# Sixty filler matmuls of a hybrid block moved from the end of the recurrence to two earlier places

## The chip, the cores and the metric

The kernel runs on one core of a Trainium2 chip. The metric is the device time of one execution in microseconds (us). The engines are named as the profile names them: PE (TensorE matmul), PEld (its weight loads), DVE (VectorE), ACT (ScalarE), POOL (GpSimd), SP (the queue that issues most loads).

## What is computed

One transformer block over 512 tokens of width 1024, all in float32. The part around the change is the mixing half:

```python
z = xn @ w_in                                  # 4640 columns, split below
y_attn = sliding_window_attention(rope(q), rope(k), v, sinks)
r, k, v, w_lo, a_lo, g_lo = split(token_shift(z[..., o3:o4], mu))
# per head, one step per token:
#   sa    = state @ (-kk_t)
#   state = state * w_t + sa (kk_t*a_t)^T + v_t k_t^T
#   y_t   = state @ r_t
merged = sigmoid(z_ga) * (y_attn @ proj_attn) + sigmoid(z_gr) * (y_rwkv @ proj_rwkv)
h = x + merged @ w_out
```

Behind it come a normalisation and a product-key expert layer (scores, top 16, gathered experts), which take most of the time and are not touched.

## The kernel before, in words

**Projections.** The columns of `w_in` are cut into 36 tiles of 128. `z_tile` (L767) computes one: 8 slices of the width, each as three matmuls on split operands (`steps`, L761: low by high, high by low, high by high), so 24 matmuls of 128x512 with moving operand `xh`/`xl`, into one of two PSUM tiles named `mm`. Its weights come in two halves through `weights` (L130): a load on SP's queue into `wraw` (4 buffers), a copy on ACT (`wh` or `wxh`, L139), and the remainder on POOL or DVE (`wl` or `wxl`, L140). Two sets of `wh`/`wl` and two of `wxh`/`wxl` rotate, so a weight half is prepared when PE has left the fourth half before it. `weights` stands under a raised priority.

**Recurrence.** The eight heads are four pairs (`NPAIR`), the 512 tokens eight chunks of 64. For a pair `c`:
- `z_part` (L1138) projects `kT`, `rT`, `vT` (two buffers each). The end of each tile is `shifted` (L1110): an ACT copy out of PSUM into `zt` (two buffers, L1117, raised priority), a DVE subtraction into `zd` (one buffer, L1119), and a DVE multiply-add into `kT`, `rT` or `vT` (L1120).
- `lora_part`, `norm_part` (L1146, L1162) make decay, rate and norm: small matmuls, ACT tanh, and a POOL power between two small DVE steps (`head_rsqrt`, L1095).
- `expand` (L1166): four transposes (L1107), then some 15 DVE operations, 6 POOL operations (L1190, L1200, L1201) and ACT exponentials that end in `SA`, `BK`, `BH`.
- `gram` (L1204): transposes of `vT` (L1213), products of `BK` and `SA` (L1227) that DVE masks into `PB` and `SA` (L1235, L1236), more products (L1240, L1251, L1254, L1258, L1259), and DVE's `XY` and `bon` (L1243 to L1256).
- `levels` (L1263): five doubling levels, each two rounds of matmuls (L1275, L1289) with DVE in between (`V1`, L1278; `XY`, L1292). `expand(c + 1)` is issued inside the third.
- `chain` (L1295): eight chunk steps, each four small rounds of matmuls (L1317, L1323, L1329, and the read L1309, L1311) with DVE and ACT copies between them.
- `fin1`, `fin2`, `fin3` (L1336 to L1358): group normalisation of the pair's output, a chain PE, DVE, ACT, PE, DVE, POOL, DVE, PE, DVE. `fin2` and `fin3` of pair `c` are issued in the `gram` stage of pair `c + 1`; those of the last pair stand at the end.

**Order.** In `phase_mix` PE's order is the order of the program text (a manual schedule for PE alone). DVE, ACT, POOL and SP are ordered by a planner from priorities and estimated times. PE's waits are filled by hand: `filler` (L869) is a generator that yields after each projection matmul but the last of a sum, and `F(n)` (L887) takes `n` such steps. A tile of 24 matmuls is 23 steps, since its last matmul goes with the next tile's first. The filler's order: `z_part(1)`, two `gate_r` tiles, `z_part(2)`, two `gate_r`, `z_part(3)`, four more `gate_r`, eight `gate_a` (the first five with 12 matmuls of `proj_attn`; the last three are projections alone, 72 matmuls in 69 steps). `need(c)` (L883) drives it until pair `c` is projected. After attention (132 steps) the text before has `expand(0)`, `F(24)`, and per pair: 2 steps in `gram`, 2 and 11 behind it, 3 and 4 in each of five levels, 3 and 3 in each chain step (no second 3 in the last), and 6 and 6 around `fin1`. Then `F(FE)` with 6, `fin2` of the last pair, `drain(fill)` (all that is left), and `fin3`.

**Behind it** `merge` (L208) first issues 36 matmuls of `proj_attn` for three late tiles (L219 to L221, from `yaTh`/`yaTl`), and then the `proj_rwkv` matmuls, which need all four pairs' `yrh`/`yrl`.

Of the kernel before, what the change touches and what calls it, by code (L numbers as in the profile page):

```python
# [29 lines left out]
NPAIR = 4  # L30
# [59 lines left out]
def hybrid_block_kernel(ctx, tc, a, out, dbg=None):  # L90
# [54 lines left out]
    with tc.tile_pool(name="xp", bufs=1, reuse_waits="tile") as xp:  # L145
        xh = xp.tile([P, KD, T], F32R, name="xh")
        xl = xp.tile([P, KD, T], F32R, name="xl")
        with ExitStack() as st:
            st.enter_context(tc.manual_schedule(engines={mybir.EngineType.PE}))
            phase_mix(tc, a, dump, mm3, split, ident, mhalf, ps, weights, xh, xl, mga, tgr, rstd_rows)  # L150
# [595 lines left out]
def phase_mix(tc, a, dump, mm3, split, ident, mhalf, ps, weights, xnh, xnl, mga, tgr, rstd_rows):  # L746
    nc = tc.nc
    V, S, G, PE = nc.vector, nc.scalar, nc.gpsimd, nc.tensor
    with ExitStack() as st:
# [7 lines left out]
        def drain(gen):  # L757
            for _ in gen:
                pass
# [123 lines left out]
        def need(c):  # L883
            while c not in ready:
                next(fill)

        def F(n):  # L887
            for _ in range(n):
                next(fill, None)
# [6 lines left out]
        with tc.tile_pool(name="rp", bufs=2, reuse_waits="tile") as rp:  # L896
            rw.rp = rp
            rw.expand(0)
            F(24)
            for c in range(NPAIR):  # L900
                rw.gram(c, F)
                F(FG[0])
                if c:
                    rw.fin2(c - 1)
                F(FG[1])
                if c:
                    rw.fin3(c - 1)
                if c + 1 < NPAIR:
                    need(c + 1)
                    rw.lora_part(c + 1)  # L910
                    rw.norm_part(c + 1)
                rw.levels(c, c + 1 if c + 1 < NPAIR else None, F)
                rw.chain(c, F)
                F(FF)
                rw.fin1(c)
                F(FF)
            F(FE)
            rw.fin2(NPAIR - 1)
            drain(fill)
            rw.fin3(NPAIR - 1)  # L920
# [528 lines left out]
```

## Time and profile before

| | |
|---|---|
| median of three runs | 1825.45 us (1820.81 to 1827.6) |
| the profiled execution, its own time | 1818.6 us |
| its span in the trace | 1816.7 us |
| mean granted PE clock over the span | 0.978 of full speed |
| PE busy | 1714.3 us, 94% |
| DVE busy | 1349.0 us, 74% |
| POOL busy | 780.5 us, 43% |
| ACT busy | 720.4 us, 40% |

Times in rows are microseconds from the span's start. In a row of the timeline the columns are start, length, engine, line, operation, output and inputs, tile size, count, and in brackets the engine's idle time before it with what ended it. A matmul's length overlaps the next one's, so a rate is read from starts. A windows row gives a stretch, its length, and each engine's busy time and number of instructions, then the granted clock (1.00 is 2.4 GHz, 0.50 is 1.2 GHz), the busy share of the DMA engines and GB/s.

### The profile page before, as it was taken

To read this page: it belongs to the slowest core of one execution; us is meant where nothing else is said; L and a number is where in the kernel's file an instruction comes from. 1 tells how busy PE (TensorE), PEld (TensorE's weight loads), DVE (VectorE), ACT (ScalarE), POOL (GpSimd) and SP (SyncE) were. 2 spreads that over 40 slices of the span, in tenths; PEclk is the share of its full clock that TensorE was granted. 3 is DMA by queue.
4 is the path that set the end of the run, shared out by engine and by line. 5 is a ranking of instruction groups with operands and counts; after the bars stand their busy time and mean duration, and the time that the engine had idled before them with its cause. 6 is when DMAs were issued, how large, how long until landed. Compare 5 with 4: busy or idle time off the path is not lost.

```text
span 1816.7 us, 30025 instructions
## 1 busy us (share of the span) xinstructions
PE 1714.3 (94%) x10933; PEld 1432.8 (79%) x10933; DVE 1349.0 (74%) x2564; ACT 720.4 (40%) x1415; POOL 780.5 (43%) x634
## 2 busy tenths in 40 slices
PE   7998899899999789898799999999999999998998
PEld 6765666667778668676689999999999999997886
DVE  4667665754535999999677777677788788788886
ACT  4553132221335436666633333333333333333334
POOL 5534232311155412122255555555455555556450
PEclk9998899999999889999899999999999999999999
DMA  6221111111564225563799999999989999998864
GB/s 210 81 64 41 36 42 48 36 48 54 184 205 133 88 76 178 199 216 142 243 320 325 305 313 325 317 303 317 321 302 318 322 302 320 327 309 290 297 222 167
DMA packets 193397, 378.98 MB, mean 209 GB/s; under 512 B 18624, under 2 KB 65472, under 8 KB 190176
## 3 DMA queue, kind: packets, MB, share of 16 engines
q1 hardware_dynamic: 97344, 175.71, 28.5%
q0 software_dynamic: 36864, 134.23, 22.1%
q10 hardware_dynamic: 59040, 67.12, 10.9%
q8 instruction: 86, 1.41, 0.3%
q14 instruction: 63, 0.52, 0.1%
HBM read 342.12 MB, written 33.55 MB: 207 GB/s over the span
## 4 chain that ended last, share of the span: by engine, by line
PE 45%; DVE 3%; issue 1%; DMA 1%; ACT 0%; POOL 0%; DVEq 0%; SPq 0%; POOLq 0%; ACTq 0%
PE w L96 8%; PE w L97 8%; PE w L98 8%; PE mm L96 7%; PE mm L98 7%; PE mm L97 7%; DMA vraw<-v_t 1%; DVE al L102 1%; DVE gacc L416 1%; DVE vl L102 0%; DVE wxl L102 0%; ACT w L467 0%; DVE gt L466 0%; DMA wraw<-v_t 0%; DVE wl L102 0%
## 5 line engine op out<-in xcount | busy, mean ns | idle before, releaser
L140 POOL TENSOR_TENSOR wl<-wraw,wh 128x512 fp32r<-128x512 f32 (+1 forms) x95 | 133.1, 1401 | 347.4 <-ACT wh L139 292.8
L96 PE MATMUL w<-vh,al 128*128 128x512 f32 x678 | 265.1, 391 | 6.8 <-DVE al L102 6.7
L97 PE MATMUL w<-vl,ah 128*128 128x512 f32 x678 | 264.6, 390 | 0.0
L98 PE MATMUL w<-vh,ah 128*128 128x512 f32 x678 | 264.4, 390 | 0.0
L399 POOL DMA_INDIRECT grow<-v_t,idxV x128 | 175.8, 1373 | 185.3 <-DVE gacc L416 152.1
L352 ACT ACTIVATE big<-mm 128x384 f32<-128x384 f32 x128 | 63.0, 492 | 464.6 <-PE mm L98 372.6
L399 POOL DMA_INDIRECT grow<-u_rows,idxU x128 | 167.9, 1312 | 183.4 <-DVE grow L406 164.3
L140 DVE TENSOR_TENSOR wl<-wraw,wh 128x512 fp32r<-128x512 f32 x101 | 103.8, 1028 | 153.2 <-ACT wh L139 128.4
L96 PE MATMUL mm<-x2h,wl 128*128 128x384 f32 (+1 forms) x576 | 199.2, 346 | 7.6 <-ACT big L352 6.2
L98 PE MATMUL mm<-x2h,wh 128*128 128x384 f32 (+1 forms) x576 | 191.7, 333 | 0.0
L97 PE MATMUL mm<-x2l,wh 128*128 128x384 f32 (+1 forms) x576 | 191.7, 333 | 0.0
L139 ACT ACTIVATE wh<-wraw 128x512 fp32r<-128x512 f32 (+1 forms) x196 | 122.4, 624 | 133.1 <-PE mm L763 53.0
L416 DVE SCALAR_TENSOR_TENSOR gacc<-grow,act,gacc 128x1024 f32<-128x1024 f32 x127 | 166.2, 1309 | 2.2
L102 DVE TENSOR_TENSOR vl<-vraw,vh 128x512 fp32r<-128x512 f32 x217 | 147.8, 708 | 25.5 <-ACT vh L101 25.1
L96 PEld LDWEIGHTS w<-vh,al 128*128 128x128 f32 x678 | 127.6, 188 | 33.3 <-DVE al L102 9.9
L365 POOL TENSOR_TENSOR big<-big,gt 128x384 f32<-128x384 f32 x128 | 135.8, 1064 | 34.3 <-ACT gt L576 21.2
L406 DVE SCALAR_TENSOR_TENSOR grow<-grow,xg 128x1024 f32<-128x1024 f32 x128 | 150.1, 1217 | 0.0
L98 PEld LDWEIGHTS w<-vh,ah 128*128 128x128 f32 x678 | 127.4, 188 | 26.8
L97 PEld LDWEIGHTS w<-vl,ah 128*128 128x128 f32 x678 | 127.5, 188 | 23.0
L96 PE MATMUL mm<-x2h,wxl 128*128 128x384 f32 (+1 forms) x436 | 143.5, 329 | 0.0
L97 PE MATMUL mm<-x2l,wxh 128*128 128x384 f32 (+1 forms) x436 | 143.4, 329 | 0.0
L98 PE MATMUL mm<-x2h,wxh 128*128 128x384 f32 (+1 forms) x436 | 143.4, 329 | 0.0
(388 smaller groups left out, 3944.0 us busy)
## 6 DMA issues: line engine op xcount, KB each, us to landing
wraw<-u_t SPq DMA_DIRECT2D x256, 256.0 KB
vraw<-v_t SPq DMA_DIRECT2D x217, 256.0 KB
g_dram<-stg ACTq DMA_DIRECT2D x24, 1024.0 KB
gt<-g_dram ACTq DMA_DIRECT2D x60, 384.0 KB
wraw<-wz SPq DMA_DIRECT2D x72, 256.0 KB
wraw<-v_t SPq DMA_DIRECT2D x39, 256.0 KB
wraw<-wq SPq DMA_DIRECT2D x32, 256.0 KB
wraw<-wproj SPq DMA_DIRECT2D x16, 256.0 KB
```

The lines of the kernel that those rows point to most:

```text
L96: PE.matmul(o, ll, rh, start=start, stop=False)
L97: PE.matmul(o, lh, rl, start=False, stop=False)
L98: PE.matmul(o, lh, rh, start=False, stop=stop)
L102: V.tensor_sub(lo, src, hi.bitcast(F32))
L139: S.activation(wh[:, :, :m], raw[:, :, :m], AF.Copy)
L140: lo.tensor_sub(wl[:, :, :m], raw[:, :, :m], wh[:, :, :m].bitcast(F32))
L352: S.activation(H[e], o, AF.Gelu)
L365: G.tensor_mul(ht, ht, g[:, :, e % E2B, :])
L399: G.indirect_dma_start(out=r, out_offset=None, in_=src, in_offset=bass.IndirectOffsetOnAxis(ap=idx[:, i:i + 1], axis=0))
L406: V.scalar_tensor_tensor(r, r, 1.0, xg, op0=ALU.mult, op1=ALU.mult, accum_out=hpre[:, s:s + 1])
L416: V.scalar_tensor_tensor(gacc, r, act[:, i:i + 1], gacc, op0=ALU.mult, op1=ALU.add)
```

## The change

The text calls `F(54)` where it called `F(24)`, and `F(10)` before `levels` of the first three pairs, behind `lora_part` and `norm_part` of the next pair. The filler itself is the same, so it ends 60 steps earlier.

```diff
             rw.expand(0)
-            F(24)
+            F(54)
             for c in range(NPAIR):
                 rw.gram(c, F)
                 F(FG[0])
...
                     need(c + 1)
                     rw.lora_part(c + 1)
                     rw.norm_part(c + 1)
+                if c + 1 < NPAIR:
+                    F(10)
                 rw.levels(c, c + 1 if c + 1 < NPAIR else None, F)
                 rw.chain(c, F)
                 F(FF)
```

## Rows read from the trace of the kernel before

**Rows 1.** The page's head: the span, and the granted PE clock in 40 equal slices of 45.4 us (tenths of full speed).

```profile
span 1816.7 us, 30025 instructions
...
PEclk9998899999999889999899999999999999999999
```

**Rows 2.** The windows view: four stretches of 5 us. Columns: stretch, length, then busy time (and instructions) of PE, PEld, DVE, ACT and POOL, granted clock, DMA share, GB/s.

```profile
155.00:160.00 5.00, 0.46 (x2) 0.49 (x2) 4.91 (x5) 0.72 (x1) 4.30 (x3) 0.54 0.17 52
160.00:165.00 5.00, 4.09 (x24) 2.95 (x25) 4.91 (x8) 0.00 (x0) 0.90 (x2) 0.50 0.00 0
...
185.00:190.00 5.00, 4.39 (x67) 3.42 (x65) 1.43 (x4) 0.63 (x1) 0.00 (x0) 0.66 0.13 49
...
210.00:215.00 5.00, 4.67 (x20) 2.71 (x20) 1.69 (x6) 1.33 (x3) 0.78 (x1) 0.50 0.16 52
```

**Rows 3.** PE's timeline around the first pair's `gram`.

```profile
152.46 0.60 PE L1213 MATMUL w<-ident,vT 128*128 128x128 f32 x4
159.54 0.76 PE L1227 MATMUL w<-SA,BK 64*128 64x128 f32 x2 [6.48 <-DVE BK L1199]
161.22 2.04 PE L1227 MATMUL w<-SA,BK 64*128 64x128 f32 x14 [0.91 <-DVE BK L1199]
```

**Rows 4.** DVE's timeline in the same stretch: the end of `expand(0)`, and the first and last masked product of `gram(0)`.

```profile
153.59 1.75 DVE L1198 TENSOR_TENSOR BK<-kk,encum 64x512 f32<-64x512 f32 x1
...
157.04 0.69 DVE L1198 TENSOR_TENSOR BK<-kk,encum 64x512 f32<-64x512 f32 x1
157.76 3.31 DVE L1199 TENSOR_TENSOR BK<-av,encum 64x512 f32<-64x512 f32 x2
...
163.33 0.67 DVE L1235 TENSOR_TENSOR PB<-w,mgram 64x512 f32<-64x512 f32 x1
...
171.19 0.67 DVE L1256 TENSOR_TENSOR bon<-w,vT 128x512 f32<-128x512 f32 x1
```

**Rows 5.** POOL's timeline there: two weight remainders, the second with POOL's idle time before it.

```profile
154.87 1.59 POOL L140 TENSOR_TENSOR wl<-wraw,wh 128x512 fp32r<-128x512 f32 x1
...
173.47 1.28 POOL L140 TENSOR_TENSOR wxl<-wraw,wxh 128x512 fp32r<-128x512 f32 x1 [10.46 <-ACT wxh L139]
```

**Rows 6.** PE's timeline in the levels: five rounds that PE waited for (pair 0 in the first three, then pair 1 and pair 2).

```profile
184.53 0.68 PE L1275 MATMUL w<-XY,PB 64*64 64x64 f32 x16 [2.85 <-DVE XY L1292]
...
185.82 0.88 PE L1275 MATMUL w<-XY,PB 64*64 64x64 f32 x16 [0.61 <-ACT cum L1184]
...
208.40 1.15 PE L1289 MATMUL w<-XY,V 64*64 64x64 f32 x32 [1.85 <-DVE V L1278]
...
265.08 0.68 PE L1275 MATMUL w<-XY,PB 64*64 64x64 f32 x16 [1.55 <-DVE XY L1292]
...
342.31 1.37 PE L1275 MATMUL w<-XY,PB 64*64 64x64 f32 x32 [3.03 <-ACT lw L1181]
```

**Rows 7.** DVE's timeline in the levels of pair 0: the preparation of pair 1, the first `XY`, and the token shift of pair 2's `vT`.

```profile
179.56 1.48 DVE L1101 COPY hw<-hv 128x512 f32<-128x512 f32 x1 [0.51 <-POOL hv L1099]
180.97 1.75 DVE L1180 TENSOR_TENSOR lw<-cum,lw 128x512 f32<-128x512 f32 x1
...
183.79 0.68 DVE L1292 TENSOR_TENSOR XY<-w,XY 128x512 f32<-128x512 f32 x1
...
193.25 1.33 DVE L1119 TENSOR_TENSOR zd<-zt 128x512 f32<-128x512 f32 x1
```

**Rows 8.** PE's timeline at the end of the recurrence: last chain step, `fin1`, `fin2`, `fin3`'s transposes, and `merge`'s first `proj_attn` and first `proj_rwkv` matmul.

```profile
457.54 0.33 PE L1323 MATMUL w<-U,XY 64*64 64x64 f32 x4
...
460.71 1.02 PE L1342 MATMUL w<-yT,blk 128*128 128x512 f32 x2
...
464.56 0.95 PE L1091 MATMUL w<-blk,fin 128*128 128x2 f32 x8
...
475.02 0.60 PE L1107 MATMUL w<-ident,hw 128*128 128x128 f32 x4
475.37 0.48 PE L96 MATMUL w<-yaTh,wxl 128*128 128x512 f32 x1
...
483.86 0.40 PE L96 MATMUL w<-yrh,wl 128*128 128x512 f32 x1
```

**Rows 9.** The windows view of the filler's line (L763) alone, from the last chain step to `merge`, and of `drain(fill)`. Columns: stretch, length, busy time and number of PE and PEld, granted clock, DMA share, GB/s.

```profile
457.54:475.37 17.83, 15.98 (x64) 11.79 (x64) 1.00 0.47 152
465.37:475.02 9.65, 9.65 (x42) 7.78 (x42) 1.00 0.72 237
```

**Rows 10.** DVE's timeline at the end of the recurrence.

```profile
458.17 0.23 DVE L1325 COPY UV<-w 64x64 f32<-64x64 f32 x1 [0.68 <-ACT UV L1324]
461.77 0.69 DVE L1343 SCALAR_TENSOR_TENSOR yT<-w,yT 128x512 f32<-128x512 f32 x1 [3.38 <-PE w L1342]
465.55 0.17 DVE L1098 TENSOR_SCALAR hv<-w 128x8 f32<-128x8 f32 x1 [3.08 <-PE w L1091]
467.46 0.63 DVE L1101 COPY hw<-hv 128x512 f32<-128x512 f32 x1 [1.75 <-POOL hv L1099]
...
479.87 0.68 DVE L102 TENSOR_TENSOR yrl<-yr,yrh 128x512 fp32r<-128x512 f32 x1
```

**Rows 11.** ACT's timeline there: the square of `fin1`.

```profile
462.49 0.63 ACT L1345 ACTIVATE fin<-yT 128x512 f32<-128x512 f32 x1 [2.06 <-DVE yT L1343]
```

**Rows 12.** POOL's timeline there: the power of `fin2`.

```profile
465.79 1.63 POOL L1099 TENSOR_TENSOR hv<-hv,mhalf 128x8 f32<-128x8 f32 x1 [0.38 <-DVE hv L1098]
```

## The prediction, made before the changed kernel ran

> **What bounds the kernel now.** I read the page's head first: PE's granted clock is at its upper level nearly all the time, and the slices below it lie in the first quarter and a few places later [rows 1]. The windows view of the first quarter says where: about 155 to 165 us, 185 to 190 and 210 to 215 the granted clock is 0.50 to 0.66, each time at or behind a stretch in which PE stood [rows 2]. PE's timeline then names the waits. In front of `gram(0)` PE stands 6.48 and 0.91 us for the last `BK` of `expand(0)` [rows 3], and DVE, which makes it, is busy 4.91 of every 5 us there [rows 2]: `expand(0)` and `gram(0)` are paced by DVE. In the levels PE waits for DVE's `XY` or `V1` again [rows 6]. At the end of the recurrence it is the other way round: the granted clock is 1.00, filler matmuls stand back to back (42 in `drain(fill)`, 9.65 us or 0.23 us each, 64 in all from the last chain step to `merge`) [rows 9], and the normalisation chain runs hidden beneath them. So PE bounds the end, DVE the two places to which the change brings work.
>
> **What moves.** 60 filler steps are nearly 63 matmuls (24 matmuls are 23 steps): 31 at `F(54)`, 10.4 at each `F(10)`, 63 fewer at the end. At 0.23 us that is 7.1 us, three times 2.4 us, and 14.4 us. The change removes no work; it can gain only as far as the moved matmuls fall into waits, and as far as what they leave behind can close up. Of the 64 fillers behind the last chain step one or two are left.
>
> **F(54).** PE now comes to the transposes of `vT` at 159.5 instead of 152.46, and to the first `BK` product at about 160.1; its two operands were there at 159.54 and 161.22 [rows 3]. The 7.1 us fit into 7.4 us of waiting. The lower clock that followed costs nothing today, since DVE goes from `BK` through the masked products (163.33) to `bon` (171.19) without a gap that PE caused [rows 4]; curing it gains nothing. What is moved along: PE leaves two weight halves some 15 us earlier, so SP's loads, ACT's copies and POOL's remainders come earlier. POOL's remainder at 173.47, after 10.46 us of idle POOL, and the next one would then fall into 154 to 162 [rows 5], beside the `BK` products. Of two equal `BK` products the one took 1.75 us and the other 0.69 us [rows 4], so a collision costs DVE 1.06 us. From below the cost is zero (POOL's work lands between DVE's operations; a gain is excluded, as DVE has no idle time to close). From above DVE stands for both remainders, 1.59 and 1.28 us [rows 5], and does the token shift's subtraction for `rT(2)` in front of `BK` (0.69 us, as the short `BK`): 3.6 us. I take one collision, **+1.1 us**.
>
> The Trainium skill (SBUF — State Buffer, Who interferes with whom) says that a VectorE instruction with two SBUF inputs and a GpSimd one that reads SBUF exclude each other for a whole instruction; by that both remainders count in full and this term would be +2.9 us. The rows show the stretch of 1.06 us but not what lay on POOL at each start, so the sum keeps 1.1.
>
> **Token shifts.** With 40 more steps done by the end of `levels(0)`'s entry, the shift of `vT(2)` (1.33 us for its subtraction, in the DVE-paced third level [rows 7]) falls to the neighbourhood of `gram(0)`. Its targets are free only late: `rT(2)` overwrites `rT(0)`, read by L1254 in `gram(0)`, and `vT(2)` overwrites `vT(0)`, read by `bon` at 171.19 [rows 4]. PE doesn't wait for this, because ACT's copy empties `mm` first. DVE's relief in the third level on is set against the wait of 1.85 us there [rows 6] and the 5 us at the lower clock behind it [rows 2], worth 2.5 us: at best -4.4, at worst 0 (the planner fills the room with other work of `expand(1)`). I take **-1.5 us**, a third, since 1.33 us is less than the wait.
>
> **F(10), three times.** Each puts 2.4 us of PE work between `norm_part(c + 1)` and the first level. What is queued behind it is the level's matmuls, and DVE's `V1` and `XY` for them; meanwhile DVE can do the preparation of the next pair, which today stands in front of the first `XY` (`hw` 1.48, `lw` 1.75 us, then `XY` at 183.79) [rows 7]. Pair 0: the waits are 2.85 and 0.61 us [rows 6], and at 0.66 in 185 to 190 [rows 2] two thirds of 5 us run at half rate, which costs 1.7. Best 2.4 - 5.2 = -2.8; worst +2.4, if DVE keeps its order and only starts later. I take **-1.5**: most of the wait and half the clock. Pair 1: 1.55 us of wait [rows 6], no clock: between +0.9 and +2.4, I take **+0.9**. Pair 2: 3.03 us [rows 6], like pair 0: best 2.4 - 3.0 - 1.7 = -2.3, worst +2.4, I take **-1.5**.
>
> **The end.** The cover goes, so what is late next is the chain itself, and PE's order makes `merge`'s 36 `proj_attn` matmuls wait behind `fin3`'s transposes. From L1323 at 457.54 [rows 8], by starts: `UV` copied at 458.40 [rows 10]; the read and its ACT copy some 0.9 (an estimate: a small round of 0.33 us [rows 8] and twice the 0.23 us of such a copy [rows 10]); L1342 to DVE 1.06 [rows 8, 10]; to ACT's square 0.72 [rows 10, 11]; the square 0.63 and a hand-over 0.1; L1091 to DVE 0.99 [rows 8, 10]; to POOL 0.24 [rows 10, 12]; to `hw` 1.67 [rows 10, 12]; `hw` 0.63 and 0.1; L1107 to L96 0.35 [rows 8]. With the 0.86 to 458.40 that is 8.2 us, against 17.83 us today: -9.6 us. `yrl` of the last pair came 4.0 us before its first use [rows 8, 10] and moves with `fin3`, so the second half of `merge` waits for nothing new.
>
> Two costs come off it. PE works for some 3 of these 8 us, and behind the wait of 6.48 us its clock was 0.54 and then 0.50 all through 160 to 165, although PE was busy for 4.09 of 5 us [rows 2, 3]. So the chain's own matmuls take about 1 us more, and the `proj_attn` matmuls run some 5.5 us at half rate, 2.7 us lost; twice that as a bound. And weight remainders for `merge`, now early, can stand in front of a DVE step of the chain: one, 0.7 us, by the like `yrl` [rows 10]. **-9.6 + 3.7 + 0.7 = -5.2 us**, between -9.6 and -2.5.
>
> The Trainium skill (TensorE: Matmul & The Clock Gate, Loop structure matters more than you think) speaks against this part: bursts separated by waits run at the lower of the two rates, matmuls standing back to back do not. By it the 2.7 us are due; without it the end would give 7.9.
>
> **The sum.** 1.1 - 1.5 - 1.5 + 0.9 - 1.5 - 5.2 = -7.7 us on the profiled execution's 1818.6 us (span 1816.7), so 1810.9. That execution lies 6.85 us under the median of 1825.45, and I carry the difference over: 1817.8 us. All best ends give -18.2, all worst +8.3. Behind 484 us PE stays the pace until the top-16 work, and that waits for scores, so I let the shift pass on whole. A measurement of this kernel tells some 0.5%, 9.1 us, from no change.
>
> **Rivals.**
> - *Clock and waits both cured*: the planner uses each 2.4 us for the next pair's preparation, the levels' waits and their slow stretches go, the shift of `vT(2)` pays 3 us. 0 - 2.8 + 0.9 - 2.3 - 3 - 5.2 = -12.4: 1813. For it: DVE has the preparation at hand when `norm_part` is through. Against: those orders come from estimates, and POOL's power stands in the middle of the preparation (0.51 us of DVE's wait [rows 7]). Chance 0.25.
> - *Slower: DVE's order in the levels stays.* Place: DVE's queue behind the first `V1`. If `hw` and `lw` stay queued behind `V1`, DVE waits 2.4 us longer for L1275 and then does the same work before `XY`, so every `F(10)` is paid in full. 3.6 + 7.2 + 0 - 5.2 = +5.6: 1831. It decides from the point where two of the three levels keep the wait. For it: `V1` is raised in priority. Against: `V1` can't be planned before PE delivers it. Chance 0.15.
> - *The filler can't be moved at no cost*: ACT's copy of `vT(2)` into `zt` needs the shift of `kT(2)` to be over; if it is queued ahead of ACT's `UV` copies, DVE's first steps of `gram(0)` stand some 3 us (an estimate: from the transposes, now at 160, to the first masked product's 163.33 [rows 4], by which that shift is over), and with the relief gone the sum is -7.7 + 3 + 1.5 = -3.2: 1822. Chance 0.10.
>
> The forecast has 0.50. Range: down to all-best, 1807; up, since the slower rival holds 0.15, to 1829. Faster by over 0.5% takes the first rival and a little of the forecast's tail: 0.31. Slower by as much needs the slower rival near all its worst ends: 0.09. Within: 0.60.
>
> **What would show it.** In the changed trace: no wait above 1 us before L1227 of pair 0 and a clock of 1.00 there; the first-level waits of pairs 0 and 2 under 1 us; 63 fewer L763 matmuls behind the last L1323, 8 to 10 us from there to the first L96, and a granted clock near 0.5 in it. It is wrong if L1227 of `gram(0)` starts later than about 163, if the levels' waits are as long as before, or if the end closes up to more than 13 us.

## The result, and the profile after

The change makes the kernel slower: 1832.07 us (median of 13 runs, 1830.21 to 1840.29) beside 1821.79 us for the kernel before (13 runs, 1818.63 to 1827.6), a ratio of 1.0062 with a 95% interval of 1.0049 to 1.0074. That is some 11 us, outside the predicted range and of the other sign. The span of the profiled execution is 1829.1 us, 12.4 us over that of before.

Behind the two added lines the line numbers of this kernel are 2 higher than before (L1107 is L1109, L1278 is L1280, L1289 is L1291); the experiments keep the old ones.

The granted PE clock of the kernel after in 40 slices, from the page's head, beside [rows 1]:

```profile
PEclk9999989999899989999799999999999999999999
```

Four slices lie below nine tenths, five did before, and they are others: this view doesn't show the loss. Where the time went is read from PE's first matmul of each stage. The table gives each stage's length before and what it is longer in the changed kernel and in six experiments (worked out from the starts in PE's timeline; stages run from the first `expand(0)` transpose over each pair's first L1151, L1317 and L1342 to the last chain step's L1323 and the first `yrh` matmul). Four of the executions measured for the experiments were slower by far, the profiled one of e10 (F(10) in pair 0) among them at 5814.03 us; the ratios leave them out, and the column for pair 0 is read from e15, the same kernel.

| stage | before, us | after | F(54) | three F(10) | F(10), pairs 1 and 2 | F(10), pair 0 | F(34) | F(34), fin2 raised |
|---|---|---|---|---|---|---|---|---|
| expand(0), gram(0) | 28.2 | +3.6 | +3.5 | -0.1 | +0.6 | +0.5 | +0.2 | +0.3 |
| lora to chain, pair 0 | 36.6 | +2.7 | -2.3 | +5.3 | +0.1 | +3.9 | -0.6 | -0.7 |
| chain 0 | 27.7 | -0.4 | +2.4 | +1.8 | -2.2 | +3.0 | +1.9 | +1.1 |
| gram(1) | 16.9 | +3.0 | +0.8 | +3.5 | 0 | +2.2 | +3.4 | +0.6 |
| lora to chain, pair 1 | 33.7 | +3.2 | +1.4 | +5.9 | +7.0 | +5.5 | +5.7 | +4.4 |
| chain 1, gram(2) | 42.4 | +0.4 | 0 | -0.9 | -0.8 | -0.8 | -0.8 | -0.7 |
| lora to chain, pair 2 | 36.6 | +2.5 | -0.2 | +4.4 | +0.6 | -1.5 | -0.6 | -1.6 |
| chain 2 to the last step | 89.2 | +0.7 | +0.1 | +0.1 | +1.0 | +1.8 | +1.8 | +1.8 |
| the end, to `yrh` | 26.3 | -5.7 | -6.4 | -6.4 | -4.7 | -2.3 | -2.3 | -2.2 |
| sum | | +10.0 | -0.7 | +13.6 | +1.6 | +12.3 | +8.7 | +3.0 |

The other 2.4 us of the span after lie ahead of `expand(0)` (1.2) and behind the first `yrh` matmul (1.2), in parts that the change leaves alone.

How far can one trace of each kernel be compared? e14, which moves no matmul, has each of these stages within 0.5 us of before, but is 1.1 us longer ahead of them and 2.1 behind. And chain 0 of the run with F(10) in pairs 1 and 2 (e7) is 2.2 us shorter, though nothing ahead of it on PE was moved: behind a wait of 1.85 us in both, the granted clock is 1.00 in 213 to 218 there, and 0.50 in 210 to 215 before [rows 2]. So a difference of 2 us in one stage can be the clock alone.

**The levels.** PE's timeline of the kernel after, at its three longest waits between 175 and 475 us, beside [rows 6] (start, length, engine, line, operation, tiles, size, count; in brackets the idle time before and what ended it):

```profile
189.53 0.48 PE L1291 MATMUL w<-V,XY 64*64 64x64 f32 x4 [3.62 <-DVE V L1280]
...
264.75 1.08 PE L1109 MATMUL w<-ident,hw 128*128 128x128 f32 x4 [3.11 <-DVE hw L1103]
...
356.30 0.48 PE L1291 MATMUL w<-V,XY 64*64 64x64 f32 x4 [4.27 <-DVE V L1280]
```

The waits of pairs 0 and 2 did not go, they moved: in place of 2.85 and 0.61 us for `XY` PE stands 3.62 us for `V` (the rows' name for `V1`), in pair 2 4.27 us in place of 3.03. The third wait, 3.11 us in `gram(1)`, has no counterpart before. DVE's timeline in the first level of pair 0, beside [rows 7], says why the first moved:

```profile
184.23 1.49 DVE L1103 COPY hw<-hv 128x512 f32<-128x512 f32 x1 [1.16 <-POOL hv L1101]
185.64 1.75 DVE L1182 TENSOR_TENSOR lw<-cum,lw 128x512 f32<-128x512 f32 x1
...
189.07 0.74 DVE L1280 TENSOR_TENSOR V<-w,lvl 128x256 f32<-128x256 f32 x2
```

PE came to the level's first round at 183.87, some 2.4 us later than without F(10). On DVE `hw`, `lw`, `lam` and `cum` now follow one another from 184.23 to 189.15, and `V` stands behind them, though PE's round is over at 185.02. Before, the same preparation stood between `V1` and `XY`.

**The clock behind the waits** (windows view of the kernel after: stretch, length, busy time of PE, PEld, DVE, ACT and POOL, granted clock, DMA share, GB/s), beside [rows 2]:

```profile
190.00:195.00 5.00, 5.00 (x66) 4.18 (x62) 1.38 (x2) 0.00 (x0) 0.00 (x0) 0.50 0.09 35
265.00:270.00 5.00, 5.00 (x17) 3.15 (x17) 2.90 (x7) 1.26 (x2) 0.00 (x0) 0.50 0.00 0
474.42:484.69 10.27, 5.28 (x31) 3.73 (x29) 3.23 (x7) 3.96 (x9) 3.12 (x3) 0.71 0.41 125
484.69:488.67 3.98, 3.98 (x11) 3.12 (x10) 3.10 (x6) 0.00 (x0) 0.39 (x1) 0.50 0.21 78
```

Behind the waits of 3.62 and 3.11 us the granted clock is 0.50, the lower of its two levels (1.2 GHz); PE is busy all of 190 to 195 and 265 to 270. In the second stretch `lora_part` and the head sums run at half rate, and most of F(10) in it and behind it: from `lora_part` to the first level it takes 8.4 us (265.77 to 274.21) where it took 2.0 without F(10)'s 2.4.

**gram(0).** ACT's, DVE's and POOL's timeline of the kernel after, beside [rows 4]:

```profile
164.85 0.60 ACT L1119 ACTIVATE zt<-mm 128x512 f32<-128x512 f32 x1 [3.51 <-DVE kT L1122]
...
165.99 1.56 ACT L1219 ACTIVATE UV<-w 64x256 f32<-64x256 f32 x4
```

```profile
159.03 3.37 DVE L1201 TENSOR_TENSOR BK<-av,encum 64x512 f32<-64x512 f32 x2
...
162.43 1.65 DVE L1204 SCALAR_TENSOR_TENSOR rT<-rT,vec,av 128x512 f32<-128x512 f32 x1
164.00 0.74 DVE L1122 SCALAR_TENSOR_TENSOR kT<-zd,vec,zt 128x512 f32<-128x512 f32 x1
...
166.79 1.81 DVE L1220 COPY W<-UV 64x512 f32<-64x512 f32 x2 [1.26 <-ACT UV L1219]
168.53 0.67 DVE L1237 TENSOR_TENSOR PB<-w,mgram 64x512 f32<-64x512 f32 x1
```

```profile
161.93 1.60 POOL L140 TENSOR_TENSOR wxl<-wraw,wxh 128x512 fp32r<-128x512 f32 x1
...
166.62 1.26 POOL L140 TENSOR_TENSOR wxl<-wraw,wxh 128x512 fp32r<-128x512 f32 x1
```

For the kernel before, two of DVE's operations that no group above shows:

```profile
161.10 0.75 DVE L1202 SCALAR_TENSOR_TENSOR rT<-rT,vec,av 128x512 f32<-128x512 f32 x1
...
162.55 0.85 DVE L1218 COPY W<-UV 64x512 f32<-64x512 f32 x2
```

PE waits only 0.54 us at the `BK` products, and the last `BK` is done 14.9 us after `expand(0)` began, as before (14.8). But DVE's first masked product starts 21.1 us after `expand(0)` began; before it was 17.1 (163.33) [rows 4]. Of these 4.0 us the rows show 1.9 beside weight remainders on POOL: L1204 takes 1.65 us for 0.75, the two `W` copies 1.81 for 0.85. Between `kT` and `W` lie 0.69 us for the next shift's subtraction (164.84) and 1.26 us in which DVE waits for `UV`: ACT's copy of `vT(2)` into `zt` stands 3.51 us for `kT`, with the `UV` copies queued behind it.

**gram(1).** POOL's and DVE's timeline:

```profile
260.82 1.28 POOL L140 TENSOR_TENSOR wl<-wraw,wh 128x512 fp32r<-128x512 f32 x1 [10.67 <-ACT wh L139]
262.06 2.08 POOL L1101 TENSOR_TENSOR hv<-hv,mhalf 128x8 f32<-128x8 f32 x1
```

```profile
258.36 0.68 DVE L1121 TENSOR_TENSOR zd<-zt 128x512 f32<-128x512 f32 x1
...
260.77 0.15 DVE L1100 TENSOR_SCALAR hv<-w 128x8 f32<-128x8 f32 x1
260.88 1.77 DVE L1122 SCALAR_TENSOR_TENSOR vT<-zd,vec,zt 128x512 f32<-128x512 f32 x1
264.18 0.43 DVE L1103 COPY hw<-hv 128x512 f32<-128x512 f32 x1 [1.53 <-POOL hv L1101]
```

A weight remainder of 1.28 us stands on POOL ahead of fin2's power `hv`, and token shifts stand on DVE around it. For the kernel before the same places, which no group above shows:

```profile
252.88 1.63 POOL L1099 TENSOR_TENSOR hv<-hv,mhalf 128x8 f32<-128x8 f32 x1 [6.97 <-DVE hv L1098]
255.80 1.27 POOL L140 TENSOR_TENSOR wxl<-wraw,wxh 128x512 fp32r<-128x512 f32 x1 [1.28 <-ACT wxh L139]
```

```profile
252.66 0.14 DVE L1098 TENSOR_SCALAR hv<-w 128x8 f32<-128x8 f32 x1
254.55 0.43 DVE L1101 COPY hw<-hv 128x512 f32<-128x512 f32 x1 [1.75 <-POOL hv L1099]
```

There the power began 0.1 us after its input and took 1.63 us; from `hv`'s start on DVE to the end of `hw` it took 2.3 us. After the change it is 3.8 us, and the shifts (0.73 and 0.68 us, L1122 and L1121) lie ahead of it too.

**The end.** PE's timeline of the kernel after, beside [rows 8]:

```profile
474.42 0.33 PE L1325 MATMUL w<-U,XY 64*64 64x64 f32 x4
...
483.92 1.11 PE L1109 MATMUL w<-ident,hw 128*128 128x128 f32 x4 [2.70 <-DVE hw L1103]
484.69 0.78 PE L96 MATMUL w<-yaTh,wxl 128*128 128x512 f32 x1
485.26 0.63 PE L97 MATMUL w<-yaTl,wxh 128*128 128x512 f32 x1
485.69 0.63 PE L98 MATMUL w<-yaTh,wxh 128*128 128x512 f32 x1
```

From the last L1323 to `merge` 10.27 us (17.83 before), 62 fewer L763 matmuls in it, then `merge` at half rate until 488.67. To the first `yrh` (495.07) it is 20.65 us in place of 26.32.

### The profile page after: what moved, and what is told of

Its sections match the earlier page's. It is cut to its first block, busy times and chain, and to the rows that moved or that the text cites. A ratio compares the mean times of both kernels' runs of the same rounds, so it can differ in the third digit from the quotient of the medians.

```text
span 1829.1 us, 30034 instructions
## 1 busy us (share of the span) xinstructions
PE 1718.4 (94%) x10933; PEld 1434.5 (78%) x10933; DVE 1350.5 (74%) x2564; ACT 719.5 (39%) x1415; POOL 782.7 (43%) x634
## 4 chain that ended last, share of the span: by engine, by line
PE 45%; DVE 2%; issue 1%; DMA 1%; ACT 1%; POOL 0%; DVEq 0%; POOLq 0%; SPq 0%; ACTq 0%
PE w L97 8%; PE w L96 8%; PE w L98 8%; PE mm L96 7%; PE mm L98 7%; PE mm L97 7%; DVE al L102 1%; DMA vraw<-v_t 1%; DVE gacc L416 1%; DVE vl L102 0%; ACT w L467 0%; DVE wxl L102 0%; DVE gt L466 0%; DVE wl L102 0%; DVE gt L476 0%
## 5 line engine op out<-in xcount | busy, mean ns | idle before, releaser
L96 PE MATMUL w<-vh,al 128*128 128x512 f32 x678 | 265.4, 391 | 7.1 <-DVE al L102 7.1
L140 DVE TENSOR_TENSOR wl<-wraw,wh 128x512 fp32r<-128x512 f32 x101 | 96.7, 957 | 162.5 <-ACT wh L139 157.4
L96 PE MATMUL mm<-x2h,wl 128*128 128x384 f32 (+1 forms) x576 | 198.6, 345 | 7.9 <-ACT big L352 6.4
L96 PEld LDWEIGHTS w<-vh,al 128*128 128x128 f32 x678 | 127.6, 188 | 33.6 <-DVE al L102 10.4
L96 PE MATMUL mm<-x2h,wxl 128*128 128x384 f32 (+1 forms) x436 | 143.3, 329 | 0.0
```

Source lines behind the costliest of these rows:

```text
L96: PE.matmul(o, ll, rh, start=start, stop=False)
L140: lo.tensor_sub(wl[:, :, :m], raw[:, :, :m], wh[:, :, :m].bitcast(F32))
```

## The experiments

Ratios are to the kernel before, run on the same chip beside them (medians 1820.36, 1820.12, 1820.16 and 1820.48 us for the four groups).

| run | median, us | ratio, 95% interval |
|---|---|---|
| e1 F(54) alone | 1821.09 | 1.0005 (0.9996 to 1.0014) |
| e2 three F(10) alone | 1832.19 | 1.0062 (1.0049 to 1.0075) |
| e3 F(50) alone | 1823.37 | 1.0008 (0.9993 to 1.0024) |
| e4 F(54), third `zt` | 1821.03 | 0.9994 (0.9983 to 1.0005) |
| e5 F(10) ahead of `lora_part` | 1838.37 | 1.0096 (1.0081 to 1.0111) |
| e6 F(10) inside the first level | 1833.36 | 1.0077 (1.0055 to 1.0099) |
| e7 F(10), pairs 1 and 2 | 1824.04 | 1.0021 (1.0010 to 1.0033) |
| e8 whole change, `fin2` raised | 1833.82 | 1.0077 (1.0058 to 1.0095) |
| e9 F(34) alone | 1830.45 | 1.0052 (1.0037 to 1.0067) |
| e10 F(10), pair 0 | 1835.16 | 1.0078 (1.0062 to 1.0093) |
| e11 F(54), third `zt`, `fin2` raised | 1820.88 | 1.0000 (0.9989 to 1.0011) |
| e12 F(44), third `zt` | 1823.72 | 1.0022 (1.0011 to 1.0032) |
| e13 F(34), `fin2` raised | 1829.08 | 1.0051 (1.0037 to 1.0065) |
| e14 `fin2` raised alone | 1820.20 | 1.0001 (0.9992 to 1.0011) |
| e15 e10 once more | 1833.52, one run | |

### Which half loses: e1 and e2

```diff
 e1
-            F(24)
+            F(54)
 e2
+                F(10 if c + 1 < NPAIR else 0)
                 rw.levels(c, c + 1 if c + 1 < NPAIR else None, F)
```

> Only F(24) to F(54); no F(10). Theory (ACT queue): the copy of vT(2) into zt stands on ACT ahead of the UV copies and waits for the shift of kT(2), so gram(0) is late by about 3.5 us at L1151 of pair 1 against the kernel before, as in the changed kernel; the end keeps some 33 fillers, nearly the length of its chain, and gives back about 7 us: -3 us in all, so the loss of the change sits with F(10). Rival (position of the filler): the 30 steps alone bring the shifts of rT(3) and vT(3) into gram(1), PE waits some 3 us for L1107 there and works at the lower clock behind it: +3 us in all.

> Only the three F(10); F(24) stays. Theory (DVE order): the planner puts the next pair's preparation (hw, lw, lam, cum) ahead of V1 on DVE, so PE's wait in each first level comes back in front of L1289 as long as before (3 to 4 us for pairs 0 and 2) and each F(10) is paid in full: 7 us before the end, 7 us less at the end, 0 in all (within 2 us). Rival (the F(10) fill the waits as predicted): first-level waits under 1 us, and -8 us in all.

The loss is the F(10)s'. F(54) alone is even with before (-3 and +3 us were forecast): it pays 3.5 us at `gram(0)`, gets 2.3 back in pair 0's levels, loses 4.6 by chain 1, and saves 6.4 at the end. The F(10)s alone bring the whole loss. Their waits for `V` are there (3.91 us in pair 0, 3.43 in pair 2), but so is a wait of 3.14 us at L1107 in `gram(1)`, and they are 20.0 us late at the last chain step. Neither theory had that total.

### gram(0): e3 and e4

```diff
 e3
-            F(24)
+            F(50)
 e4, with F(54)
-... name="zt", bufs=2)
+... name="zt", bufs=3)
```

> F(24) to F(50), four steps fewer than the change, no F(10): the tile of vT(2) does not end before gram(0), and the planner's order on ACT has the UV copies ahead of the next zt copy. Theory (ACT queue): the first masked product of gram(0) starts about 3 us earlier, relative to expand(0), than with F(54); PE's lateness at L1151 of pair 1 is 1.5 us or less in place of 3.5; in all 2 us faster than with F(54) alone. Rival (POOL's weight remainders slow expand(0) and gram(0)): no difference to F(54) beyond 0.5 us, since the same weight halves are prepared in that stretch.

> F(54) alone with three zt buffers for two: ACT's order stays as with F(54), but the copy of vT(2) no longer has to wait for the shift of kT(2). Theory (ACT queue): the UV copies come right behind the transposes, DVE's idle time in front of the W copies goes, and gram(0) gets about 3 us back: some 3 us faster than F(54) alone. Rival (POOL's remainders, DVE itself): no difference beyond 0.5 us.

Both free ACT's queue as meant. In e3 the `UV` copies come at 162.95 and L1258 of `gram(0)` is 1.2 us late rather than 3.0; but `lora_part(1)` is then 4.5 us late (3.5 with F(54)), at a clock of 0.52 in 175 to 180. In e4 the `UV` copies come at 161.86, and DVE never waits for them. Yet its first masked product (167.77) starts 20.8 us after `expand(0)` began, 0.2 us earlier than with F(54) alone. DVE's and POOL's timeline say why:

```profile
165.03 2.81 DVE L1218 COPY W<-UV 64x512 f32<-64x512 f32 x2
```

```profile
164.38 1.77 POOL L140 TENSOR_TENSOR wl<-wraw,wh 128x512 fp32r<-128x512 f32 x1
166.11 1.45 POOL L140 TENSOR_TENSOR wxl<-wraw,wxh 128x512 fp32r<-128x512 f32 x1
```

The `W` copies, earlier now, run beside two remainders and take 2.81 us where they took 0.85. PE waits 2.67 us at L1251, `lora_part(1)` is 6.0 us late, and chain 0 3.8. So ACT's order doesn't hold `gram(0)` back by itself: without it DVE loses nearly the same time beside POOL's remainders. The whole times, 1823.37 and 1821.03 us beside 1821.09 of e1, show no gain, as the rivals had it.

### Where the F(10) stands: e5 and e6

```diff
 e5
-                    rw.lora_part(c + 1)
+                    F(10); rw.lora_part(c + 1)
 e6, between V1 and L1289 of the first level
-            F(FV)
+            F(FV + (10 if l == 0 and nxt is not None else 0))
```

> The three F(10) alone, moved in front of lora_part of the next pair, so that the next pair's preparation is not at hand while they run; F(24) stays. The planner's order on DVE has V1 ahead of hw and lw again. Theory (DVE order): PE's wait in front of L1289 of the first level (3.91 us in pair 0 with F(10) behind norm_part) is gone, the wait for XY of 2.9 us is back, and the start of pair 0's chain is late by 2 to 3.5 us against the kernel before, in place of 5.2. Rival (any 10 fillers ahead of the level cost the same): late by 5 us as before.

> The same three times ten steps put where PE stands: inside the first level, between V1 and L1289 (F(13) for F(3) there), pairs 0 to 2; F(24) stays. Theory (it is the place, not the number): in pair 0 the waits of 2.85 and 0.61 us for XY shrink below 1 us and the clock stays up, pair 0's chain starts no later than 0.5 us after that of the kernel before, the 6.4 us come off the end, and it is 3 to 8 us faster than before in all. Rival (60 fillers fewer at the end simply turn up in front of it; DVE takes every bit of time it is given): late by 5 us at pair 0's chain and no gain in all.

In pair 0 both do what the theories expected: the wait for `V` goes (e5 has 1.56 and 0.61 us for `XY`, e6 the two rows below), and in e6 chain 0 begins 0.7 us early with a granted clock of 1.00 in all the levels. PE's timeline of e6:

```profile
186.50 1.37 PE L1275 MATMUL w<-XY,PB 64*64 64x64 f32 x32 [0.96 <-DVE XY L1292]
...
189.81 0.33 PE L1289 MATMUL w<-V,XY 64*64 64x64 f32 x4 [1.05 <-DVE V L1278]
...
260.22 1.09 PE L1107 MATMUL w<-ident,hw 128*128 128x128 f32 x4 [3.14 <-DVE hw L1101]
```

Yet e5 is slower than e2 and e6 no faster (3 to 8 us faster than before was expected of it), and both stand over 3.1 us at L1107 in `gram(1)`. So the matmuls' place in the first level explains the moved wait and not the loss.

### How much hangs on pair 0, and on fin2: e7 and e8

```diff
 e7
+                F(10 if c in (1, 2) else 0)
 e8, with the whole change
-                    rw.fin2(c - 1)
+                    with tc.high_priority(offset=2 * PRE): rw.fin2(c - 1)
```

> F(10) for pairs 1 and 2 only, so that the filler stands up to gram(1) where it stood before. Theory (position of the filler): PE's wait of 3.1 us for L1107 in gram(1), which the filler's shift brings by a weight remainder on POOL ahead of the power and a token shift on DVE, is not there; pair 1's first level starts 2.5 us late in place of 16.8, and in all 4 to 5 us are lost against 11 with all three. Rival (the wait comes with F(10) in that pair, whatever stood before): the wait is there and the first level starts 9 us late.

> The whole change, with fin2 of the earlier pair under a raised priority: on POOL the power of gram(1) then stands ahead of the weight remainder, and on DVE its hv ahead of the last XY steps. Theory (that queue is the cause of the wait for L1107 and of the low clock behind it): the wait of 3.11 us falls under 1.2 us, the clock stays up, pair 1's first level starts 5 to 7 us earlier, and 5 to 7 us of the loss of 10 are back. Rival (F(10) pays by DVE's preparation in any case, and the wait for L1107 is hidden slack): under 2 us back.

Without F(10) in pair 0 two thirds of the loss go: +3.8 us (1.0021), near the 4 to 5 forecast, with waits for `V` of 3.56 and 2.97 us and no wait over 1 us at L1107 in `gram(1)`. In e8 POOL's power comes ahead of the remainder, L1107 waits 1.31 us in place of 3.11, and the first level of pair 1 begins 6 us earlier than in the kernel after, as expected; then PE stands 4.63 us for `V` there, chain 1 begins 13.3 us late (12.1 after the change), and the time is no shorter than that of the change. The rival, that DVE paces this stretch, holds for the total.

### The filler's position alone: e9 to e12

```diff
 e9
-            F(24)
+            F(34)
 e10
+                F(10 if c == 0 else 0)
 e11: F(54), zt with 3 buffers, fin2 as in e8
 e12: F(44), zt with 3 buffers
```

> F(34) in place of F(24) behind expand(0), nothing in front of the levels: from gram(0) on the filler is 10 steps ahead, as it is behind the first level with F(10) in pair 0, but pair 0's levels hold no extra matmul. Theory (the position of the filler alone makes weight remainders and token shifts meet fin2's power in gram(1)): PE waits about 3 us there at L1107 for DVE's hw, lora_part(2) to the first level of pair 1 takes about 8 us in place of 2.0, the milestones are 6 to 10 us late by level 1; the end gives back 2.4 us; total +4 to +8 us. Rival (the wait comes from pair 0's levels having been disturbed): no wait over 1 us at L1107 in gram(1), milestones within 2 us up to the last chain step, total -2.4 to 0 us.

> F(10) in front of the levels of pair 0 alone. Theory (position of the filler): everything that three F(10) do up to the first level of pair 1: V1 waited for about 3.6 us in pair 0, chain 0 at about +5, L1107 in gram(1) waited for about 3 us, level 1 at +14 to +17; total +5 to +9 us, most of the loss of three F(10) (+12) and more than F(10) for pairs 1 and 2 together cost (+3.9). Rival (each F(10) is simply paid, 2.4 us each and a little clock): total 0 to +2 us, L1107 under 1 us.

> F(54) with a third zt buffer and fin2 of the former pair at a raised priority, no F(10). Theory (the power behind a weight remainder is a wait of its own): the L1107 wait of 1.82 us that F(54) has in gram(1) goes and the kernel is 1 to 3 us faster than F(54) with three zt buffers, -2 to -4 us against the kernel before. Rival (DVE paces these stages, a wait that goes in gram comes back in the level): the time of F(54) with three zt buffers, -1 us against before.

> F(44) with a third zt buffer: 20 steps (4.7 us) moved into the 7.4 us of waiting in front of gram(0) instead of 30. Theory (what is paid at gram(0) is the order of ACT's and DVE's work behind a filler that is too far on, and PE's own slow clock): gram(0) costs nothing, the products of BK start no later than before, the end gives back some 4 us, total -2 to -4 us. Rival (any shift of the filler's position re-deals the weight remainders in gram and levels): a wait of 2 to 3 us appears somewhere in gram(1) to level 2 and the total is -1 to +5 us.

e9 settles the main question, whether the filler's position alone can cost the loss. It puts nothing into any level and 10 steps (2.4 us) into a wait of 6.48 us, where they cost 0.2 us, and is slower by 0.52%. POOL's, DVE's and PE's timeline of e9 in `gram(1)`, and its clock there:

```profile
255.33 1.88 POOL L140 TENSOR_TENSOR wxl<-wraw,wxh 128x512 fp32r<-128x512 f32 x1 [12.33 <-ACT wxh L139]
257.16 2.08 POOL L1099 TENSOR_TENSOR hv<-hv,mhalf 128x8 f32<-128x8 f32 x1
259.21 1.26 POOL L140 TENSOR_TENSOR wl<-wraw,wh 128x512 fp32r<-128x512 f32 x1
```

```profile
255.98 0.15 DVE L1098 TENSOR_SCALAR hv<-w 128x8 f32<-128x8 f32 x1
256.09 1.67 DVE L1120 SCALAR_TENSOR_TENSOR rT<-zd,vec,zt 128x512 f32<-128x512 f32 x1
259.28 1.48 DVE L1101 COPY hw<-hv 128x512 f32<-128x512 f32 x1 [1.52 <-POOL hv L1099]
```

```profile
260.90 1.09 PE L1107 MATMUL w<-ident,hw 128*128 128x128 f32 x4 [3.18 <-DVE hw L1101]
```

```profile
260.00:265.00 5.00, 4.10 (x13) 2.30 (x14) 2.51 (x4) 0.97 (x2) 0.47 (x1) 0.51 0.17 52
265.00:270.00 5.00, 5.00 (x53) 4.12 (x55) 3.17 (x7) 0.89 (x3) 1.61 (x1) 0.50 0.00 0
```

The tile boundary comes 10 steps earlier, so ACT's copy of the weight half does too, and its remainder starts on POOL 0.8 us ahead of the end of `hv`, for which fin2's power waits. From `hv`'s start to the end of `hw` it is 4.8 us in place of 2.3: the power starts 1.0 us after its input, runs 2.08 us beside the token shift (1.63 before), and `hw` takes 1.48 us beside the next remainder (0.43 before). PE stands 3.18 us, and the clock is at its lower level for ten microseconds. The first level of pair 1 is entered 6.6 us late, as expected, though lora to it takes 3.8 us and not 8: the slow clock falls into the level's first rounds instead, and that stage is 5.7 us longer. The end gives 2.3 us back, as expected of 10 steps. The total, +9.5 us, is over the +4 to +8 expected.

e10 is F(10) in pair 0 alone: +14 us, no less than all three together, and over the expected +5 to +9. So the F(10) of pairs 1 and 2 cost nothing once pair 0 has its own, and cost 3.8 us without it: the terms don't add.

e11 is even with before, like e4: where L1107 waits 1.81 us (e4) and 1.09 (e11) the raised `fin2` buys nothing, as its rival had it. e12's theory fell: `gram(0)` is only 1.1 us late at L1258 and chain 0 is early by 1.5, but PE waits 1.98 us at L1107 in `gram(1)` and 3.04 in pair 1's first levels, and it is 0.22% slower. Its rival was right.

### One order on POOL: e13 to e15

```diff
 e13, with F(34); e14, without
-                    rw.fin2(c - 1)
+                    with tc.high_priority(offset=2 * PRE): rw.fin2(c - 1)
 e15: e10 once more
```

> F(34) with fin2 of the former pair at a raised priority: against F(34) alone POOL's power of gram(1) comes ahead of the weight remainder instead of behind it, and DVE's copy hw ahead of half of the token shift; PE's and ACT's order stays. Theory (this one order on POOL makes the wait of 3.18 us at L1107, the slow clock behind it and the loss of F(34)): the wait falls under 1.3 us, lora_part(2) to the first level of pair 1 takes 2 to 4 us in place of 8.5, chain 1 begins 3 us late at most in place of 10.6, and the kernel takes -1 to +3 us against the kernel before, 6 us or more under F(34). Rival (the wait only shows what the next pair's preparation on DVE and POOL sets anyway; what goes in gram(1) comes back in level 1): L1107's wait goes, the next level's wait grows by as much, chain 1 begins 8 us late or more, total +7 to +10 us as F(34).

> The kernel before with fin2 of the former pair at the raised priority alone, for the kernel above: only gram(2) changes its order on DVE (hv and hw some 1 us earlier). Both theories: L1107's wait of 0.78 us in gram(2) goes, total -1 to +1 us; the rest of the stages as before.

> F(10) in front of the levels of pair 0 alone once more, for its trace. Theory: V1 waited for 3 to 4 us in pair 0, L1107 of gram(1) about 3 us behind DVE's hw, with a weight remainder ahead of the power on POOL; granted clock near 0.5 behind it, the level of pair 1 entered 14 to 17 us late; chain 1 to chain 3 hold that lateness. Rival: the lateness comes in steps of 2 to 3 us at several places.

In e13 POOL's order in `gram(1)` is that of the kernel before again. POOL's and PE's timeline:

```profile
253.87 2.02 POOL L1099 TENSOR_TENSOR hv<-hv,mhalf 128x8 f32<-128x8 f32 x1 [11.50 <-DVE hv L1098]
255.85 1.26 POOL L140 TENSOR_TENSOR wxl<-wraw,wxh 128x512 fp32r<-128x512 f32 x1
```

```profile
257.54 0.63 PE L1107 MATMUL w<-ident,hw 128*128 128x128 f32 x4 [1.53 <-DVE hw L1101]
...
269.01 1.97 PE L1275 MATMUL w<-XY,PB 64*64 64x64 f32 x32 [3.68 <-ACT lw L1181]
```

L1107 waits 1.53 us in place of 3.18, `gram(1)` runs at a clock of 1.00, and lora to the first level takes 2.0 us in place of e9's 3.8 (the 8.5 in the expectation is that of the whole change). But the second wait above is 3.68 us where it was 1.84 in e9: it grew by about as much as the first fell, as the rival had it. Its row names ACT's `lw`, which ends at 268.93; DVE's first `XY`, which the round reads, ends at 268.87. DVE's timeline shows what kept both, again a preparation ahead of the level's own work:

```profile
265.12 1.48 DVE L1101 COPY hw<-hv 128x512 f32<-128x512 f32 x1 [1.46 <-POOL hv L1099]
266.52 1.75 DVE L1180 TENSOR_TENSOR lw<-cum,lw 128x512 f32<-128x512 f32 x1
268.19 1.28 DVE L1292 TENSOR_TENSOR XY<-w,XY 128x512 f32<-128x512 f32 x2
```

Both `XY` stand behind `hw` and `lw`; in the kernel before the first `XY` went ahead of `hw` (261.40 and 262.95), and PE waited 1.55 us [rows 6]. Chain 1 begins 5.7 us late, between the two theories. The time is the rival's: +9.3 us (1.0051), as e9, with intervals that overlap almost wholly. Its profiled execution doesn't account for that: at the first `yrh` 5.7 of e9's 8.7 us are gone, and of its 8.3 us over the span of before only 3.0 lie in the stages of the table, 5.3 ahead of them and behind. There traces differ without a reason in the edit: those of e4 and e11, whose stages add up alike, by 2.8 us behind the first `yrh`. So the order on POOL makes the wait and the slow clock in `gram(1)`; that taking it back makes the kernel faster isn't shown, as in e8, and where e13 loses the rest isn't either.

e14 has the time of before, and its wait of 0.78 us at L1107 in `gram(2)` is gone, as both theories said. e15 is one execution, of 1833.52 us: PE stands 3.92 us for `V` in pair 0 and 3.17 us at L1107 in `gram(1)`, where a remainder (260.52) lies ahead of the power (262.38). The first level of pair 1 begins 11.0 us late, less than the 14 to 17 expected; chains 1 to 3 hold 12.8 to 15.1. The lateness before that comes in steps of 2 to 4 us, so the rival has part of it.

## Why the prediction was wrong

**F(54), +1.1 us.** The wait was filled as forecast: the last `BK` moved by 0.1 us only, and the first product of `BK` started at 161.52, at a clock of 1.00 in 160 to 165. The term was too small: the stage is 3.6 us longer. The collision with weight remainders came on two later operations, L1204 and `W`, at 0.9 and 1.0 us, and the shift's subtraction of 0.69 us came with it; that is nearly what the term's worst end held (3.6). The third rival's copy into `zt` came too, and DVE's 1.26 us of waiting behind it. But e4, which takes that away, is no earlier at the first masked product than by 0.2 us, as DVE then stands beside POOL's remainders. With F(54) alone the last chain step is 5.7 us late, and the 6.4 us at the end pay it back (e1).

**Token shifts, -1.5 us.** The room was there: with F(54) alone pair 0's levels are 2.3 us shorter (e1), some 1 us of it since `lam` took 0.16 us (187.12) where it had taken 1.23 (182.65) beside a weight remainder. But the prediction never asked where the shifts and weight halves of pair 3 would land. In `gram(1)` they land at fin2: that stage has +3.0 us, and `lora_part`, the head sums and F(10), which at the full rate take 2.0 and 2.4 us, take 8.4 with the slow clock behind it. No term of the sum stood for this. The sum asked of collisions only at `gram(0)` and at the end, where the filler's matmuls moved, though every later tile boundary moves with them. e9, with 10 steps moved and nothing else, shows that the position alone can cost +9.5 us. Through which orders, the runs show in part: the remainder ahead of the power makes the wait of 3.1 us and the slow clock behind it, but with that order taken back (e8, e13) DVE's next wait grows and the time stays.

**F(10), -1.5, +0.9 and -1.5 us.** The step that failed is "meanwhile DVE can do the preparation of the next pair". DVE did it, but `V` then stood behind it, and the waits moved from `XY` to `V` and grew: 3.62 for 2.85 and 0.61, 4.27 for 3.03. The stages are longer by 2.7, 3.2 and 2.5 us. For pairs 0 and 2 that looks like the slower rival's price, an F(10) paid in full, though by another order than it named (it kept `hw` and `lw` behind `V1`). But without F(54) the same stages are 5.3 and 4.4 us longer (e2), and pair 2's 0.6 in e7: an F(10) is no fixed price, as e6 and e10 show too. The rival's 1831 us is near the 1832.07 measured by luck: its +5.6 us stood on 1825.45 us, the median of three runs, and on the 1821.79 of thirteen it gives 1827.4. Its 3.6 us for `gram(0)` came; it lacks the 3.0 us of `gram(1)`, and its +2.4 us for pair 1 is a stage that pays for the slow clock too.

**The end, -5.2 us.** Right: -5.7 us. The chain to `merge` took 10.27 us, a quarter of a microsecond over the 8 to 10 forecast. `merge` behind it ran at 0.50 for 3.98 us, with matmuls 0.43 us apart (485.26 to 485.69), and from L96 to `yrh` it is 10.38 us where it was 8.49 [rows 8]: 1.9 us lost, where 2.7 was priced. The Trainium skill (TensorE: Matmul & The Clock Gate, Loop structure matters more than you think) has matmuls run at the lower rate behind waits; the trace agrees here, and behind the waits of 3.62 and 3.11 us.

**The sum.** In the traces -7.7 was forecast, +12.4 came: the end had its size, and what stands ahead of it came to +15.7 at the last chain step where -2.5 was summed. Of the prediction's three signs of being wrong one came, and it was enough: the levels' waits were as long as before.

What stays open: why the stage from lora to chain of pair 1 is 4.4 us longer in e13, where `gram(1)` runs at the full clock. The rows of e13 show DVE's order (`hw`, `lw`, then `XY`); no run turned that order alone. Whether another position of the filler is faster than the kernel before is open too: of the five with no F(10) and 20 to 30 steps moved, none was.

## What to carry to other kernels

A filler drawn from a queue isn't a stretch of matmuls that can be put elsewhere: what it draws along (weight copies, remainders, evictions) moves at every later place, and so must be priced at each short chain that it can meet, above all one that hops between two engines. Where another engine's order is planned, a wait that is filled on PE is not gone; look at what that engine will put ahead of the next product that PE needs. Move the smallest part alone first (here ten steps into a wait that could hold them): its time shows whether the position or the work costs.

## What the runs showed of the hardware

DVE's copy `hw` of 128x512 takes 0.43 us with POOL idle (254.55 before) and 1.48 us beside a weight remainder (259.28 in e9): 3.4 times as long. Two `W` copies of 64x512 take 0.85 us with no weight remainder beside them (162.55 before) and 2.81 beside two (165.03 in e4). POOL's power of 128x8 takes 1.63 us with DVE idle and 2.08 beside L1120 of the token shift (257.16 in e9). The Trainium skill (SBUF — State Buffer, Who interferes with whom) says that a copy can enter a mode in which VectorE and GpSimd shut each other out; the two lengths of `hw` agree with it, and no run here shows the mode itself.
